# Norm factors spread over the partitions by a transfer and GpSimd instead of TensorE transposes, with the kernel's end regrouped by token blocks

## The chip, the core and the metric

One core of a Trainium2 chip runs the whole program. The metric is the time of one execution on the device in microseconds (us); lower is better. The engines are TensorE (PE in profiles, its weight loads PEld), VectorE (DVE), ScalarE (ACT), GpSimd (POOL) and SyncE (SP, which here only issues transfers).

## What is computed

Two layers of a bidirectional encoder over 512 tokens of 1024 channels, float32, and a last RMSNorm:

```python
def rmsnorm(x, g):
    y = xf * lax.rsqrt(jnp.mean(xf * xf, axis=-1, keepdims=True) + EPS)
    return (y * g).astype(x.dtype)

for l in range(DEPTH):                      # 2
    h = rmsnorm(x, norm1_g[l])
    x = x + gated_parallel_mixer(h, w_in[l], ...)   # three attentions, gates, w_out
    h = rmsnorm(x, norm2_g[l])
    x = x + conv_ffn(h, w_up[l], conv_w[l], conv_b[l], w_down[l])
return rmsnorm(x, final_g)
...
kv = (rmsnorm(c_kv, g_kva) @ w_ukv)         # inside the latent attention (also for c_q)
```

## The kernel before, in words

**Layout.** Activations lie with channels on the 128 partitions and the 512 tokens along the row, so `x` is eight tiles of 128x512. Every weight tile (512 KB at most) comes from HBM on SP's queue into `raw`, is split by ACT into a rounded high part `whi` (L148) and by DVE into the rest `wlo` (L149), and each product is three float32r matmuls per 128 channels, high by high, high by low, low by high (`mm3`, L162 to L164). Three tiles of `raw` and of `whi`/`wlo` are in flight. A matmul of a `wlo` waits for DVE, so whatever stands ahead of an L149 in DVE's queue can hold PE.

**Norms are applied late.** A norm's factor is one number per token. The matmuls run on unscaled input, and DVE multiplies the result by the factors as it leaves PSUM. For that the 512 factors must stand along the row, and the same on all 128 partitions. `rs_tokens` (L185 to L201) adds up the squares over the partitions: four transposes on PE (L191), a reduction on DVE (L193), and small operations on GpSimd (L195 to L200, a power of -0.5 among them). Its result `rt` is 128x4: token 128j+p sits on partition p, column j. `rs_spread` (L203) turns `rt` into the tile `rb` or `rbk`, 128x512: four more transposes on PE of a column repeated 128 times (L208) into one PSUM bank, and a copy by ACT (L209).

**Where `rs_spread` is called.** Three times in a layer, six in all:
- the first norm (`do_lat`, by `norm_spread`): `rb`, first read by DVE in `do_kr` (`ev<-ev,rb`, L155);
- the latent norm (`do_rb_k`): `rbk`, first read in `do_kn(0)` (`ev<-ps_d,rbk`, L155), whose result is split into `kn` (L148, L149) for the scores of `do_ms` (L505 to L509);
- the second norm (`do_up`): `rb`, first read by `conv` (`u<-ps_g,rb`, L155), while PE goes on with further `w_up` tiles.

**Order of the work.** PE's and SP's orders are written out by hand (the list in `schedule`, under `manual_schedule`). The orders on DVE, ACT and GpSimd come from the Tile scheduler, with the weight splits (`fetch`) and the attention steps raised in priority. Each engine works strictly in its order.

**The end.** In the last layer `do_down(1)` hands its last three weight tiles to `finish`. There, for channel tiles m = 1, 2, 3 and halves of 256 tokens, `product` runs 18 matmuls, adds into `x` (DVE L947), squares (ACT L948), adds the squares up (DVE L950) and applies the gain (DVE L951). `total` sums the squares over the partitions by a matmul with a column of ones (L960), `scales` forms mean and power -0.5 on DVE and GpSimd (L965, L967), `turn` transposes 128x128 blocks so that tokens come onto partitions (L955), and `emit` scales two 128x512 halves on ACT and DVE (L971, L972) and sends the rows out (L975 to L978). Token blocks 0 and 1 leave while the last two half products run; blocks 2 and 3 end the program.

Of the kernel before, what the change touches and what calls it, by code (L numbers as in the profile page):

```python
# [10 lines left out]
F32 = mybir.dt.float32  # L11
F32R = mybir.dt.float32r
BF16 = mybir.dt.bfloat16
AF = mybir.ActivationFunctionType
ALU = mybir.AluOpType
AX = mybir.AxisListType

P = 128
L = 2
D = 1024  # L20
S = 512
# [3 lines left out]
EPS = 1e-6  # L25
# [17 lines left out]
def r32(ap):  # L43
    return ap.bitcast(F32)
# [14 lines left out]
class Trunk:  # L59
# [143 lines left out]
    def rs_spread(self, rt, rb):  # L203


        ps = self.bank("r")
        for j in range(4):
            self.nc.tensor.transpose(ps[:, j * P:(j + 1) * P], rt[:, j:j + 1].to_broadcast([P, P]), self.idf)  # L208
        self.nc.scalar.copy(rb, ps)  # L209

    def rope(self, pool, ps, rows, ct, st, nb=2):
        nc = self.nc
# [508 lines left out]
    def do_gq_open(self):  # L721
        nc = self.nc
        self.nps.close()
        self.banks(d=[0, 1], s=[2, 3], tp=[4, 5, 6], po=[7])
        self.gps_, self.gp = self.open("gq")
        gp = self.gp
        rope = gp.tile([P, 2, S], F32, tag="yf", name="rope")
        self.rc, self.rsn = rope[:, 0, :], rope[:, 1, :]
        nc.gpsimd.dma_start(self.rc, self.d["rope"][:, :S])
        nc.gpsimd.dma_start(self.rsn, self.d["rope"][:, S:])  # L730
        self.mul(self.rc, self.rc, self.rb)
        self.mul(self.rsn, self.rsn, self.rb)
        self.sink = self.pr[:, PC_SINK:PC_SINK + 8]
        self.nsink = self.small.tile([P, 8], F32, tag="nsink", name="nsink")
        nc.vector.tensor_scalar(self.nsink, self.sink, -1.0, None, ALU.mult)
        self.gqs = {}

# [154 lines left out]
    def do_down(self, g):  # L892
        nc = self.nc
        if g == 0:
            self.banks(g=[0, 1, 2, 3])
        else:
            self.banks(g=[4, 5, 6, 7])
        ps = [self.bank("g") for _ in range(4)]
        last = self.l == L - 1
        if g == 0 and not last:  # L900
            nc.scalar.activation(self.warm, r32(self.ff[-1][0])[:, 0:1], AF.Exp, scale=0.0)
            self.norm_begin()
        if g == 0 and last:
            self.acc, self.ntags, self.xg = None, ["acc", "sq0", "sq1"], []
        for i, spec in enumerate(self.W["down", g]):
            m, k0, nk = i % 4, spec[1] // P, spec[2]
            if last and (g, k0, m) == (1, 16, 1):
                self.finish([self.weights(sp) for sp in self.W["down", 1][i:]], self.ff[k0:k0 + nk])
                break
            tail = last and g == 1 and m > 0  # L910
            self.mm3(ps[m], self.weights(spec), self.ff[k0:k0 + nk], k0 == 0, k0 == (8 if tail else 16))
            if tail and k0 == 8:
                nc.vector.tensor_add(self.x[4 + m], self.x[4 + m], ps[m])
            if k0 == 16:
                k = 4 * g + m
                nc.vector.tensor_add(self.x[k], self.x[k], ps[m])
                if last:
                    self.acc = self.sumsq(self.const, self.x[k], self.acc, self.ntags)
                    xg = self.const.tile([P, S], F32, tag=f"hh{k}", name="xg")
                    nc.scalar.activation(xg, self.x[k], AF.Copy, scale=self.pr[:, PC_FIN + k:PC_FIN + k + 1])  # L920
                    self.xg.append(xg)
                else:
                    self.norm_piece(k, self.par[self.l + 1][:, PC_G1:PC_G1 + 8])
        if g == 1:
            self.fps.close()

    def finish(self, sts, mv):

        nc = self.nc
        self.banks(z=[1, 2, 3], a=[0, 4, 5, 6], r=[7, 7, 1])
        ps = [None] + [self.bank("z") for _ in range(3)]
        fin = self.pr[:, PC_FIN:PC_FIN + KD]
        for k in range(5, KD):
            self.xg.append(self.const.tile([P, S], F32, tag=f"hh{k}", name="xg"))
        sq = [self.const.tile([P, S], F32, tag=f"hl{k}", name="sq") for k in range(5, KD)]
        outs = [self.fp.tile([P, 2, S], F32, tag="o", name="o", bufs=3) for _ in range(3)]
        outs.append([self.const.tile([P, S], F32, tag=t, name="o") for t in ("hl3", "hl4")])
        rts = self.small.tile([P, 4], F32, tag="rt", name="rts", bufs=3)  # L940
        mss = self.small.tile([P, 4], F32, tag="ms", name="mss", bufs=2)

        def product(m, h):
            k, ts = 4 + m, slice(h * 256, h * 256 + 256)
            self.mm3(ps[m][:, ts], sts[m - 1], [(a[:, ts], b[:, ts]) for a, b in mv])
            x = self.x[k][:, ts]
            nc.vector.tensor_add(x, x, ps[m][:, ts])  # L947
            nc.scalar.activation(sq[m - 1][:, ts], x, AF.Square)  # L948
            if m < 3 or h == 0:
                nc.vector.tensor_add(self.acc[:, ts], self.acc[:, ts], sq[m - 1][:, ts])  # L950
            nc.vector.tensor_scalar(self.xg[k][:, ts], x, fin[:, k:k + 1], None, ALU.mult)  # L951

        def turn(j, hf, ms):
            for m in ms:
                nc.tensor.transpose(tp[j, hf][:, m * P:(m + 1) * P], self.xg[4 * hf + m][:, j * P:(j + 1) * P], self.idf)  # L955

        def total(h, i, src, last=True):
            for j in (0, 1):
                js = slice((2 * h + j) * P, (2 * h + j + 1) * P)
                nc.tensor.matmul(r[h][j][:, 0:1], src[:, js], self.ones[:, 0:1], start=i == 0, stop=last)  # L960

        def scales(h):
            for j in (0, 1):
                c = slice(2 * h + j, 2 * h + j + 1)
                nc.vector.tensor_scalar(mss[:, c], r[h][j][:, 0:1], 1.0 / D, EPS, ALU.mult, ALU.add)  # L965
            hs = slice(2 * h, 2 * h + 2)
            nc.gpsimd.tensor_tensor(rts[:, hs], mss[:, hs], self.neghalf[:, 0:2], ALU.pow)  # L967

        def emit(j):
            o = [outs[j][:, 0, :], outs[j][:, 1, :]] if j < 3 else outs[j]  # L970
            nc.scalar.activation(o[0], tp[j, 0], AF.Copy, scale=rts[:, j:j + 1])  # L971
            nc.vector.tensor_scalar(o[1], tp[j, 1], rts[:, j:j + 1], None, ALU.mult)  # L972
            rows = self.d["out"][j * P:(j + 1) * P, :]
            if j < 3:
                nc.sync.dma_start(rows, outs[j][:].rearrange("p h c -> p (h c)"))  # L975
            else:
                nc.scalar.dma_start(rows[:, :S], o[0])
                nc.sync.dma_start(rows[:, S:], o[1])  # L978

        for m in (1, 2, 3):  # L980
            product(m, 0)
        product(1, 1)
        b = self.bank("r")
        r = [[b[:, 0:S // 2], b[:, S // 2:]]]
        total(0, 0, self.acc)
        scales(0)
        tp = {(j, hf): self.bank("a") for j in (0, 1) for hf in (0, 1)}
        for j, hf in list(tp):
            turn(j, hf, range(4))
        emit(0)  # L990
        emit(1)
        product(2, 1)
        for j, hf in list(tp):
            tp[j + 2, hf] = self.bank("a")
        turn(2, 0, range(4))
        product(3, 1)
        r.append([self.bank("r") for _ in range(2)])
        turn(3, 0, range(4))
        turn(2, 1, range(3))
        total(1, 0, self.acc, False)  # L1000
        total(1, 1, sq[2])
        scales(1)
        turn(3, 1, range(3))
        turn(2, 1, (3,))
        turn(3, 1, (3,))
        emit(2)
        emit(3)


@with_exitstack  # L1010
# [63 lines left out]
```

## Time and profile before

| | before |
|---|---|
| median of 3 runs | 1707.21 us (1707.13 to 1707.24) |
| the profiled execution, its own time | 1707.45 us |
| its span, first to last instruction | 1705.7 us |
| PE busy | 1697.0 us, 99% |
| DVE, ACT, POOL busy | 1147.1, 868.2, 41.8 us (67, 51, 2%) |
| mean granted TensorE clock | 0.999 of full |
| PE waits with a releaser shown | 3 groups: 1.0, 0.8 and 0.3 us in total |

The profile is one execution. Of the 1707.45 us, 1705.7 lie between its first and last instruction, and 1.75 around them. A row of the timeline gives start, duration, engine, line, operation and operands, then in brackets how long the engine stood idle before it and what released it. Matmuls overlap, so their price is read from start to start and not from their durations.

### The profile page before, as it was taken

How to read it: one execution, taken by the hardware profiler on the slowest of the kernel's cores; microseconds unless marked ns; L12 is line 12 of the kernel's file. 1: busy time of each engine (PE TensorE's matmuls, PEld its weight loads, DVE VectorE, ACT ScalarE, POOL GpSimd, SP SyncE). 2: the span in 40 equal slices, each digit the busy share in tenths (PEclk: the TensorE clock that was granted, in tenths of full speed). 3: DMA queues.
4: the chain of work that ended last, by engine and by line, in shares of the span. 5: the costliest groups of instructions: out<-in, count | busy, mean ns of one | idle time of the engine just before them, and what ended most of it. 6: DMA issues, size and time to landing. Idle time of an engine off the chain costs nothing.

```text
span 1705.7 us, 21166 instructions
## 1 busy us (share of the span) xinstructions
PE 1697.0 (99%) x7966; PEld 1420.1 (83%) x7966; DVE 1147.1 (67%) x1873; ACT 868.2 (51%) x1505; POOL 41.8 (2%) x97
## 2 busy tenths in 40 slices
PE   9999999999999999999999999999999999999998
PEld 8888888888888888888888888888888888888887
DVE  6777875887558777734367688768766577777234
ACT  7665655775435444433266556557744444444232
POOL 1110000000000000000010100000000000000000
PEclk9999999999999999999999999999999999999999
DMA  5233233222333333333232232332223333333231
GB/s 177 78 86 82 73 103 87 75 69 74 105 95 103 98 100 99 98 88 101 80 97 79 75 90 69 108 84 69 63 80 111 106 99 99 99 93 94 85 105 68
DMA packets 289206, 155.37 MB, mean 91 GB/s; under 512 B 8816, under 2 KB 285056, under 8 KB 289104
## 3 DMA queue, kind: packets, MB, share of 16 engines
q1 hardware_dynamic: 286752, 148.92, 30.6%
q0 software_dynamic: 2064, 4.82, 0.9%
q8 instruction: 62, 1.02, 0.2%
q14 instruction: 40, 0.33, 0.1%
q10 hardware_dynamic: 288, 0.29, 0.0%
HBM read 151.89 MB, written 2.10 MB: 90 GB/s over the span
## 4 chain that ended last, share of the span: by engine, by line
PE 95%; DVE 1%; issue 1%; ACT 0%; POOLq 0%; POOL 0%; DVEq 0%
PE ps_d L162 21%; PE ps_d L163 21%; PE ps_d L164 21%; PE ps_g L162 7%; PE ps_g L164 7%; PE ps_g L163 7%; PE ps_tp L815 1%; PE ps_po L671 1%; PE ps_tp L656 1%; PE ps_tp L525 1%; PE ps_s L785 1%; PE ps_s L784 1%; PE ps_po L830 1%; PE ps_po L829 1%; PE ps_s L638 0%
## 5 line engine op out<-in xcount | busy, mean ns | idle before, releaser
L148 ACT CAST whi<-raw 128x1024 fp32r<-128x1024 f32 (+4 forms) x339 | 301.4, 889 | 594.3 <-PE ps_d L163 347.0
L162 PE MATMUL ps_d<-hh,whi 128*128 128x512 f32 x1328 | 519.5, 391 | 0.0
L163 PE MATMUL ps_d<-hl,whi 128*128 128x512 f32 x1328 | 517.9, 390 | 0.0
L164 PE MATMUL ps_d<-hh,wlo 128*128 128x512 f32 x1328 | 517.6, 390 | 0.0
L149 DVE TENSOR_TENSOR wlo<-raw,whi 128x1024 fp32r<-128x1024 f32 (+4 forms) x337 | 344.4, 1022 | 183.8 <-ACT whi L148 183.5
L164 PEld LDWEIGHTS ps_d<-hh,wlo 128*128 128x128 f32 x1328 | 249.5, 188 | 52.3
L162 PEld LDWEIGHTS ps_d<-hh,whi 128*128 128x128 f32 x1328 | 249.6, 188 | 50.6 <-DVE rot L155 0.5
L163 PEld LDWEIGHTS ps_d<-hl,whi 128*128 128x128 f32 x1328 | 249.6, 188 | 49.7
L164 PE MATMUL ps_g<-ff,wlo 128*128 128x512 f32 x334 | 130.1, 390 | 0.0
L162 PE MATMUL ps_g<-ff,whi 128*128 128x512 f32 x334 | 130.1, 390 | 0.0
L163 PE MATMUL ps_g<-ff,whi 128*128 128x512 f32 x334 | 130.1, 390 | 0.0
L155 DVE TENSOR_TENSOR u<-ps_d,rb 128x512 f32<-128x512 f32 x80 | 55.3, 691 | 65.1 <-PE ps_d L164 65.1
L155 DVE TENSOR_TENSOR gz<-ps_d,rb 128x512 f32<-128x512 f32 x48 | 33.1, 690 | 84.1 <-PE ps_d L164 84.1
L879 ACT ACTIVATE c<-u,par 128x512 f32<-128x512 f32 x88 | 71.7, 814 | 5.1 <-DVE u L155 2.8
L163 PEld LDWEIGHTS ps_g<-ff,whi 128*128 128x128 f32 x334 | 62.7, 188 | 13.1
L164 PEld LDWEIGHTS ps_g<-ff,wlo 128*128 128x128 f32 x334 | 62.7, 188 | 13.0
L162 PEld LDWEIGHTS ps_g<-ff,whi 128*128 128x128 f32 x334 | 62.7, 188 | 12.8
L149 DVE TENSOR_TENSOR pl<-ps_tp,ph 128x512 fp32r<-128x512 f32 x104 | 68.4, 683 | 3.2 <-ACT ph L148 3.0
L881 DVE SCALAR_TENSOR_TENSOR c<-u,par,c 128x511 f32<-128x511 f32 x88 | 66.0, 750 | 2.7
L885 ACT ACTIVATE c<-c 128x512 f32<-128x512 f32 x44 | 27.8, 631 | 76.6 <-DVE c L881 76.6
L880 DVE SCALAR_TENSOR_TENSOR c<-u,par,c 128x511 f32<-128x511 f32 x88 | 65.5, 745 | 0.6 <-ACT c L879 0.6
L148 ACT CAST ph<-ps_tp 128x512 fp32r<-128x512 f32 x104 | 56.8, 585 | 3.7 <-PE ps_tp L525 2.8
(283 smaller groups left out, 2585.6 us busy)
## 6 DMA issues: line engine op xcount, KB each, us to landing
raw<-in_w_in_dram SPq DMA_DIRECT2D x86, 512.0 KB, 4.0
raw<-in_w_up_dram SPq DMA_DIRECT2D x80, 512.0 KB, 3.9
raw<-in_w_down_dram SPq DMA_DIRECT2D x32, 512.0 KB, 4.3
raw<-in_w_down_dram SPq DMA_DIRECT2D x16, 384.0 KB, 3.6
raw<-in_w_in_dram SPq DMA_DIRECT2D x18, 256.0 KB, 3.0
raw<-in_w_br_mla_dram SPq DMA_DIRECT2D x16, 256.0 KB, 2.8
raw<-in_w_br_na_dram SPq DMA_DIRECT2D x16, 256.0 KB, 2.8
raw<-in_w_br_gqa_dram SPq DMA_DIRECT2D x16, 256.0 KB, 2.8
```

The costliest lines, as they stand in the source:

```text
L148: nc.scalar.copy(hi, src)
L149: nc.vector.tensor_sub(lo, src, r32(hi))
L155: self.nc.vector.tensor_tensor(out, a, b, ALU.mult)
L162: mm(ps, sh, mh, start=first and k == 0, stop=False)
L163: mm(ps, sh, ml, start=False, stop=False)
L164: mm(ps, sl, mh, start=False, stop=last and k == n - 1)
L525: self.nc.tensor.transpose(tp[:, b * P:(b + 1) * P], self.pts[h, b][:, kc * P:(kc + 1) * P], self.idf)
L656: self.nc.tensor.transpose(tp[:, i * P:(i + 1) * P], self.pts["n", h, bp][:, i // 2, (i % 2) * P:(i % 2) * P + P], self.idf)
L879: nc.scalar.activation(c, u, AF.Identity, bias=pr[:, PC_CB + fi:PC_CB + fi + 1], scale=cw[:, 1:2])
L880: nc.vector.scalar_tensor_tensor(c[:, 1:], u[:, :S - 1], cw[:, 0:1], c[:, 1:], ALU.mult, ALU.add)
L881: nc.vector.scalar_tensor_tensor(c[:, :S - 1], u[:, 1:], cw[:, 2:3], c[:, :S - 1], ALU.mult, ALU.add)
L885: nc.scalar.activation(c, c, AF.Gelu_apprx_tanh)
```

## The change

Every call of `rs_spread` now issues a transfer from GpSimd's queue that gathers the 128x4 factors into one row of 512 on partition 0, and one GpSimd instruction that copies that row to all partitions, reading it with a stride of four elements so that the tokens come out in order. The transposes (L208 before) and ACT's copy (L209) are gone. The tile of the row shares the buffer `sq0`. In the program GpSimd also gets an instruction without operands ahead of each broadcast, and another ahead of the next arithmetic on it; these name which library of GpSimd functions (0 or 1) is in use.

The end is regrouped: product 1 runs over all 512 tokens, product 3's second half is added, squared and scaled in blocks of 128 tokens, the factor is a square root on ACT and a reciprocal on DVE for each block (the power on GpSimd goes, and the Sqrt table is loaded at the start of the last `do_down`), four transposes of block 2 move behind the last product, and ACT and DVE follow a written order there. The tile `nsink` moves to another pool.

```diff
     def rs_spread(self, rt, rb):
-        ps = self.bank("r")
-        for j in range(4):
-            self.nc.tensor.transpose(ps[:, j * P:(j + 1) * P], rt[:, j:j + 1].to_broadcast([P, P]), self.idf)
-        self.nc.scalar.copy(rb, ps)
+        row = self.const.tile([P, S], F32, tag="sq0", name="row")
+        self.nc.gpsimd.dma_start(row[0:1, :], rt[:])
+        self.nc.gpsimd.partition_broadcast(rb[:].rearrange("q (j p) -> q j p", p=P),
+                                           row[0:1, :].rearrange("q (p j) -> q j p", p=P))
...
-        self.nsink = self.small.tile([P, 8], F32, tag="nsink", name="nsink")
+        self.nsink = gp.tile([P, 8], F32, tag="nsink", name="nsink")
...
+        if g == 0:
+            nc.scalar.activation(self.warm, r32(self.ff[-1][0])[:, 0:1], AF.Sqrt if last else AF.Exp, scale=0.0)
         if g == 0 and not last:
-            nc.scalar.activation(self.warm, r32(self.ff[-1][0])[:, 0:1], AF.Exp, scale=0.0)
...
-        def scales(h):
-            for j in (0, 1):
-                c = slice(2 * h + j, 2 * h + j + 1)
-                nc.vector.tensor_scalar(mss[:, c], r[h][j][:, 0:1], 1.0 / D, EPS, ALU.mult, ALU.add)
-            hs = slice(2 * h, 2 * h + 2)
-            nc.gpsimd.tensor_tensor(rts[:, hs], mss[:, hs], self.neghalf[:, 0:2], ALU.pow)
+        def scale(c, j, n=1):
+            rt = rts[:, j:j + n]
+            nc.scalar.activation(rt, c, AF.Sqrt, scale=1.0 / D, bias=eps[:, 0:1])
+            nc.vector.reciprocal(rt, rt)
...
-        for m in (1, 2, 3):
-            product(m, 0)
-        product(1, 1)
...
-        product(2, 1)
...
-        turn(2, 0, range(4))
-        product(3, 1)
...
+        product(1, slice(0, S))
...
+        for m in (2, 3):
+            product(m, half[0])
...
+        product(2, half[1])
...
+        product(3, half[1])
+        with self.tc.manual_schedule(engines={mybir.EngineType.Activation, mybir.EngineType.DVE}):
+            for j in (2, 3):
+                add(3, block[j])
+            for j in (2, 3):
+                gain(3, block[j])
+            r = {j: self.bank("r")[:, 0:1] for j in (2, 3)}
+            for j in (2, 3):
+                total(r[j], j, self.acc, True, False)
+            turn(2, 0, range(4))
+            for j in (2, 3):
+                total(r[j], j, sq[2], False, True)
+            turn(2, 1, range(4))
+            for hf in (0, 1):
+                turn(3, hf, range(4))
+            for j in (2, 3):
+                scale(r[j], j)
+            for j in (2, 3):
+                emit(j)
```

**Three places in the order of the work.** First GpSimd around the second norm of layer 0 and the first norm of layer 1. Before, where `ms` is the mean of squares, `rt` the factors and `r` two products of them:

```order
L196 TENSOR_SCALAR ms<-ms 128x4
L198 TENSOR_TENSOR rt<-ms,cst 128x4
L394 DMA rope<-in_rope_dram 128x512
L395 DMA rope<-in_rope_dram 128x512
L196 TENSOR_SCALAR ms<-ms 128x4
```

Now, with `row` the gathered factors and the bare ISA rows those that name a library:

```order
L196 TENSOR_SCALAR ms<-ms 128x4
L198 TENSOR_TENSOR rt<-ms,cst 128x4
L207 DMA row<-rt 1x128x4
L208 ISA
L208 ISA rb<-row 128x512
L394 DMA rope<-in_rope_dram 128x512
L395 DMA rope<-in_rope_dram 128x512
L196 ISA
L196 TENSOR_SCALAR ms<-ms 128x4
```

Between a norm's `rt` and the next work on GpSimd there are now a transfer, two library instructions and the broadcast.

Second, DVE from the reduction of the second norm on, where `wlo` is the low part of a weight tile and `u` the first reader of `rb`. Before:

```order
L193 TENSOR_REDUCE ms<-ps_r 128x4
L149 TENSOR_TENSOR wlo<-raw,whi 128x512 x2
L149 TENSOR_TENSOR wlo<-raw,whi 128x1024
L155 TENSOR_TENSOR u<-ps_g,rb 128x512 x2
L880 SCALAR_TENSOR_TENSOR c<-u,par_75,c 128x511
```

Now:

```order
L193 TENSOR_REDUCE ms<-ps_r 128x4
L149 TENSOR_TENSOR wlo<-raw,whi 128x512 x2
L155 TENSOR_TENSOR u<-ps_g,rb 128x512 x2
L149 TENSOR_TENSOR wlo<-raw,whi 128x1024
L880 SCALAR_TENSOR_TENSOR c<-u,par_75,c 128x511 x2
```

The two readers of `rb` have moved ahead of the first 128x1024 weight split; layer 1 moves the same way.

Third, PE behind the last product, where `cst` is the column of ones, `ps_r` the sums of squares and `ps_a` the transposed blocks. Before, with a `turn` of four ahead of the product:

```order
L955 MATMUL ps_a<-idf,xg 128x128 x7
L960 MATMUL ps_r<-cst,acc 128x1 x2
L960 MATMUL ps_r<-cst,sq 128x1 x2
L955 MATMUL ps_a<-idf,xg 128x128 x5
```

Now:

```order
L968 MATMUL ps_r<-cst,acc 128x1 x2
L965 MATMUL ps_a<-idf,xg 128x128 x4
L968 MATMUL ps_r<-cst,sq 128x1 x2
L965 MATMUL ps_a<-idf,xg 128x128 x12
```

The sums of squares stand nearer to the product's end, and all sixteen transposes of blocks 2 and 3 follow it.

## Rows read from the trace of the kernel before

**Rows 1.** The span with the mean granted TensorE clock, and the page's line of busy time (share of the span, number of instructions).
```profile
core 0: 1705.7 us, clock 0.999
...
PE 1697.0 (99%) x7966; PEld 1420.1 (83%) x7966; DVE 1147.1 (67%) x1873; ACT 868.2 (51%) x1505; POOL 41.8 (2%) x97
```

**Rows 2.** The waits of PE: waiting line, what released it, total us, times, longest us.
```profile
PE ps_r L208 <- POOL rt L200: 0.8, 1, 0.8
```

**Rows 3.** PE's timeline at the second norm of layer 0: the four transposes of the spread and the matmuls behind them.
```profile
506.81 0.60 PE L208 MATMUL ps_r<-idf,rt 128*128 128x128 f32 x4
507.16 0.48 PE L162 MATMUL ps_g<-hh,whi 128*128 128x512 f32 x1
...
507.94 0.39 PE L162 MATMUL ps_g<-hh,whi 128*128 128x512 f32 x1
```

**Rows 4.** The spread of the latent norm in layer 0: the last operation on `rt` on POOL, then PE, the last matmul before the spread, its transposes, the first matmul behind them.
```profile
55.48 0.43 POOL L200 TENSOR_TENSOR rt<-rt 128x4 f32<-128x4 f32 x1
...
54.74 0.39 PE L164 MATMUL ps_d<-whi,yal 128*128 128x512 f32 x1
55.97 0.65 PE L208 MATMUL ps_r<-idf,rt 128*128 128x128 f32 x4 [0.84 <-POOL rt L200]
56.38 0.47 PE L162 MATMUL ps_d<-mg,whi 128*128 128x512 f32 x1
```

**Rows 5.** The second norm of layer 0: POOL's last operation on `rt`; DVE's next weight split and first readers of `rb`; PE's first matmul of the first 128x1024 tile and the first that reads its `wlo`.
```profile
502.94 1.04 POOL L198 TENSOR_TENSOR rt<-ms,cst 128x4 f32<-128x4 f32 x1
...
507.86 1.23 DVE L149 TENSOR_TENSOR wlo<-raw,whi 128x1024 fp32r<-128x1024 f32 x1 [2.45 <-ACT whi L148]
509.01 1.28 DVE L155 TENSOR_TENSOR u<-ps_g,rb 128x512 f32<-128x512 f32 x2
...
512.72 0.39 PE L162 MATMUL ps_d<-hh,whi 128*128 128x512 f32 x1
...
513.17 0.39 PE L164 MATMUL ps_d<-hh,wlo 128*128 128x512 f32 x1
```

**Rows 6.** The latent norm in layer 0, DVE's first reader of `rbk` and the low part of `kn`; PE's first matmul that reads that low part.
```profile
61.18 0.68 DVE L155 TENSOR_TENSOR ev<-ps_d,rbk 128x512 f32<-128x512 f32 x1
...
62.55 0.69 DVE L149 TENSOR_TENSOR kn<-ev,kn 128x512 fp32r<-128x512 f32 x1 [0.36 <-ACT kn L148]
...
66.93 0.39 PE L506 MATMUL ps_s<-kn,qn 128*128 128x512 f32 x1
```

**Rows 7.** The latent norm in layer 1, POOL's last operation on `rt` and the same matmul of PE.
```profile
897.53 0.43 POOL L200 TENSOR_TENSOR rt<-rt 128x4 f32<-128x4 f32 x1
...
910.61 0.39 PE L506 MATMUL ps_s<-kn,qn 128*128 128x512 f32 x1
```

**Rows 8.** The first norm in layer 0: POOL's last operation on `rt`, its next work that needs arithmetic, and DVE's first reader of `rb`.
```profile
23.91 1.03 POOL L198 TENSOR_TENSOR rt<-ms,cst 128x4 f32<-128x4 f32 x1
...
43.73 0.20 POOL L195 TENSOR_TENSOR ms<-ms,r 128x4 f32<-128x4 f32 x1 [15.14 <-DVE ms L193]
...
48.24 0.68 DVE L155 TENSOR_TENSOR ev<-ev,rb 64x512 f32<-64x512 f32 x1
```

**Rows 9.** Prices near those of the new operations. Transfers (queue, count, KB each, median us from issue to landing); a group of POOL's transfer issues (count | busy us, mean ns); POOL's timeline at the program's start, with a library instruction (index 0) between the two rows; the groups of ACT's table loads.
```profile
gmf<-in_gmask_dram POOLq DMA_DIRECT2D x1, 128.0 KB, 2.7
rope<-in_rope_dram SPq DMA_DIRECT2D x2, 256.0 KB, 7.2
...
L562 POOL DMA_DIRECT2D tb<-in_rpb_dram x16 | 9.7, 612 | 157.7 <-PE ps_s L508 120.3 <-DVE tm L622 18.9 <-DVE nm L646 18.4
...
0.72 0.20 POOL masks.py:197 MEMSET idf<- 128x128 f32 x1 [0.29 <-POOLq L1062]
1.00 0.29 POOL masks.py:199 TENSOR_SCALAR_AFFINE_SELECT idf<-idf 128x128 f32<-128x128 f32 x1
...
L885 ACT ACT_TABLE_LOAD x2 | 2.6, 1283 | 3.4 <-DVE c L881 3.4
```

**Rows 10.** PE at the end: the first half product (its first matmul), the sums after four of them, and the first transposes behind the last product.
```profile
1681.41 0.28 PE L162 MATMUL ps_z<-ff,whi 128*128 128x256 f32 x1
...
1690.04 0.50 PE L960 MATMUL ps_r<-cst,acc 128*128 128x1 f32 x4
...
1696.93 0.93 PE L955 MATMUL ps_a<-idf,xg 128*128 128x128 f32 x7
```

**Rows 11.** The chain behind the last product on DVE, ACT, POOL, DVE and SP.
```profile
1697.13 0.42 DVE L947 TENSOR_TENSOR x<-x,ps_z 128x256 f32<-128x256 f32 x1 [1.25 <-PE ps_z L164]
...
1697.58 0.42 ACT L948 ACTIVATE sq<-x 128x256 f32<-128x256 f32 x1 [2.17 <-DVE x L947]
...
1698.47 0.38 DVE L965 TENSOR_SCALAR mss<-ps_r 128x1 f32<-128x1 f32 x2 [0.53 <-PE ps_r L960]
...
1698.93 0.69 POOL L967 TENSOR_TENSOR rts<-mss,cst 128x2 f32<-128x2 f32 x1 [7.31 <-DVE mss L965]
...
1699.66 1.41 DVE L972 TENSOR_SCALAR o<-ps_a,rts 128x512 f32<-128x512 f32 x2 [0.81 <-POOL rts L967]
...
1701.10 0.33 SPq L978 DMA_DIRECT2D out_dram<-o  x1
```

**Rows 12.** Small operations of one column elsewhere in the kernel (count | busy us, mean ns of one).
```profile
L797 ACT ACTIVATE nm<-par,nm 128x1 f32<-128x1 f32 x64 | 18.1, 283 | 0.0
...
L514 DVE RECIPROCAL nm<-nm 128x1 f32<-128x1 f32 x32 | 4.9, 160 | 5.6 <-ACT pt L513 5.2
```

More of the change, by code (lines that the diff above doesn't have):

```diff
@@ L940, in finish, with product, add @@
         rts = self.small.tile([P, 4], F32, tag="rt", name="rts", bufs=3)
-        mss = self.small.tile([P, 4], F32, tag="ms", name="mss", bufs=2)
-        def product(m, h):
-            k, ts = 4 + m, slice(h * 256, h * 256 + 256)
+        eps = self.small.tile([P, 4], F32, tag="ms", name="eps", bufs=2)
+        tp = {}
+        nc.vector.memset(eps, EPS)
+        def product(m, ts):
             self.mm3(ps[m][:, ts], sts[m - 1], [(a[:, ts], b[:, ts]) for a, b in mv])
-            x = self.x[k][:, ts]
+        def add(m, ts):
+            x = self.x[4 + m][:, ts]
@@ L947, in product, with gain, taken @@
             nc.vector.tensor_add(x, x, ps[m][:, ts])
             nc.scalar.activation(sq[m - 1][:, ts], x, AF.Square)
-            if m < 3 or h == 0:
-                nc.vector.tensor_add(self.acc[:, ts], self.acc[:, ts], sq[m - 1][:, ts])
-            nc.vector.tensor_scalar(self.xg[k][:, ts], x, fin[:, k:k + 1], None, ALU.mult)
+        def gain(m, ts):
+            k = 4 + m
+            nc.vector.tensor_scalar(self.xg[k][:, ts], self.x[k][:, ts], fin[:, k:k + 1], None, ALU.mult)
+        def taken(m, ts):
+            nc.vector.tensor_add(self.acc[:, ts], self.acc[:, ts], sq[m - 1][:, ts])
@@ L953, in turn @@
         def turn(j, hf, ms):
+            if (j, hf) not in tp:
+                tp[j, hf] = self.bank("a")
             for m in ms:
-                nc.tensor.transpose(tp[j, hf][:, m * P:(m + 1) * P], self.xg[4 * hf + m][:, j * P:(j + 1) * P], self.idf)
-        def total(h, i, src, last=True):
-            for j in (0, 1):
-                js = slice((2 * h + j) * P, (2 * h + j + 1) * P)
-                nc.tensor.matmul(r[h][j][:, 0:1], src[:, js], self.ones[:, 0:1], start=i == 0, stop=last)
@@ L962, in scales, with total @@
-        def scales(h):
-            for j in (0, 1):
-                c = slice(2 * h + j, 2 * h + j + 1)
-                nc.vector.tensor_scalar(mss[:, c], r[h][j][:, 0:1], 1.0 / D, EPS, ALU.mult, ALU.add)
-            hs = slice(2 * h, 2 * h + 2)
-            nc.gpsimd.tensor_tensor(rts[:, hs], mss[:, hs], self.neghalf[:, 0:2], ALU.pow)
+                nc.tensor.transpose(tp[j, hf][:, m * P:(m + 1) * P], self.xg[4 * hf + m][:, block[j]], self.idf)
+        def total(c, j, src, first, last):
+            nc.tensor.matmul(c, src[:, block[j]], self.ones[:, 0:1], start=first, stop=last)
@@ L978, in emit @@
                 nc.sync.dma_start(rows[:, S:], o[1])
-        for m in (1, 2, 3):
-            product(m, 0)
-        product(1, 1)
[L983 to L989, printed above, removed]
+        half = [slice(0, 256), slice(256, 512)]
+        block = [slice(j * P, (j + 1) * P) for j in range(4)]
+        product(1, slice(0, S))
+        for step in (add, taken, gain):
+            step(1, slice(0, S))
+        for m in (2, 3):
+            product(m, half[0])
+            for step in (add, taken, gain):
+                step(m, half[0])
+        product(2, half[1])
+        for step in (add, taken, gain):
+            step(2, half[1])
+        r = self.bank("r")
+        for j in (0, 1):
+            total(r[:, j:j + 1], j, self.acc, j == 0, j == 1)
+        scale(r[:, 0:2], 0, 2)
+        for j in (0, 1):
+            for hf in (0, 1):
+                turn(j, hf, range(4))
         emit(0)
         emit(1)
-        product(2, 1)
-        for j, hf in list(tp):
-            tp[j + 2, hf] = self.bank("a")
-        turn(2, 0, range(4))
-        product(3, 1)
[L997 to L1007, printed above, removed]
+        product(3, half[1])
[11 more added lines that the diff above has]
+            turn(2, 1, range(4))
+            for hf in (0, 1):
+                turn(3, hf, range(4))
[3 more added lines that the diff above has]
+                emit(j)
 @with_exitstack
```

## The prediction, made before the changed kernel was run

> **What bounds the kernel now.** I read the page's busy times first. PE works 1697.0 of 1705.7 us, at a granted clock of 0.999, and the next engine, DVE, 1147.1 [rows 1]. So the time is PE's list of matmuls, plus what makes PE wait, plus the tail behind its last product. Then PE's waits: behind a spread there is one, 0.8 us, in which it waits for GpSimd's `rt` ahead of L208 in layer 0's latent norm [rows 2]. Last the timelines of the places that the change touches: every instruction taken from PE's list is a gain, and every new wait of PE a loss. The profiled execution took 1707.45 us, 1.75 more than its span and 0.24 more than the median of 1707.21; I sum against it and take 0.24 off at the end.
>
> **Removed: the six spreads on PE.** At a second norm the first of the four transposes starts at 506.81 and the next matmul at 507.16, so they cost 0.35 us. Three matmuls then take 0.78 (507.16 to 507.94) [rows 3], while elsewhere two take 0.45 (512.72 to 513.17) [rows 5], three 0.68: another 0.10 goes with the spread. Six times 0.45 is 2.7 us. In layer 0's latent norm PE also stood: a matmul takes 0.23, so its predecessor from 54.74 was through at 54.97, and the transposes began at 55.97, 1.0 later; they also took 0.41 instead of 0.35 [rows 4]. With that, 3.8 us. ACT's copy goes too, at no gain: ACT is busy 51% [rows 1].
>
> **Added: a transfer and a broadcast on GpSimd.** Let G be the time from `rt` complete to `rb` complete. PE no longer waits for `rt`, but whoever reads `rb` holds DVE's queue, and a weight's low part or `kn` behind it holds PE. How large may G be before PE stands?
> - Second norm, layer 0: `rt` is complete at 503.98 (502.94 + 1.04). By the new order the two `u` (1.28) and then the 128x1024 `wlo` (1.23) run after `rb`, 2.5 us together. PE reads that `wlo` first at 513.17, and 0.45 earlier without the spread, at 512.72 [rows 5]. So `rb` has until 510.2: G may be 6.2. Layer 1 has the same order, and I take 6.2 there too.
> - Latent norm, layer 0: `rt` is complete at 55.91 [rows 4]. From the first reader of `rbk` to the end of `kn`'s low part are 2.06 us (61.18 to 63.24), and PE reads it at 66.93 [rows 6], now 1.5 earlier (1.0 + 0.41 + 0.10). G may be 7.4.
> - Latent norm, layer 1: complete at 897.96, read at 910.61 [rows 7], 0.45 earlier: G may be 10.1.
> - First norm: complete at 24.94, first read at 48.24 [rows 8]: over 20 us. GpSimd's next arithmetic comes at 43.73 [rows 8]; a load, a broadcast and a load back even at 7.2 us a load would end near 45, a microsecond late for a factor that still passes through the rest of that norm. I count nothing.
>
> What is G? The only transfer on GpSimd's queue with a landing listed needed 2.7 us for 128 KB [rows 9]; the new one is 2 KB, in pieces of 16 bytes. Below, the issue alone is 0.6; above, the slowest listed landing is 7.2 [rows 9]. I take 2.7, the same queue. The broadcast writes 512 elements a partition; a 128-wide operation there took 0.29 [rows 9], so I estimate 1.2 (below 0.2, a memset of this width; four-element powers take 1.04 [rows 5]). With 0.1 at each of two hand-overs G is 4.2 if the library instruction costs nothing more.
>
> The disputed cost is that instruction. At the program's start one with index 0 stands between a memset that ends at 0.92 and a select that starts at 1.00 [rows 9], so it cost at most 0.1, but that may be the library already present. The nearest load of code or tables is ACT's table load, 1.28 us [rows 9]. Bounds: 0.1 and, as a fetch from memory, 7.2, the slowest landing. I take 1.3. In GpSimd's list it stands between the transfer's issue and the broadcast, so I expect it to run while the transfer flies: G = 2.05 + load when the load is the longer (issue 0.6, broadcast 1.2, hand-overs), and 4.2 for anything under 2.2. Then no PE stall anywhere: 2.0 us are left at the second norms.
>
> GpSimd's other work behind the broadcast is late by G: the rope transfers of layer 1, whose values are not read before the next layer, and memsets ahead of later attentions. Its 41.8 us of work in the whole span [rows 1] leave room. The load back to library 0 stands ahead of the next norm's first small operation, hundreds of us before the second norms need it. I count nothing for either.
>
> [...]
>
> **The end.** Four half products take 8.63 us (1681.41 to 1690.04), 2.16 each [rows 10]. Product 1 over 512 columns is six times three matmuls at 0.68, 4.08 instead of 4.32: 0.24 saved. Four transposes move from ahead of the last product to behind it, 0.35 by [rows 3]. Together 0.6. Behind the last product, whose end I set at 1696.93, SP issues the last rows at 1701.10 [rows 11], 4.17 later. Between the squares (end 1698.00) and the outputs stand sums, two scalings, and the power on GpSimd, which ends at 1699.62. Now a root on ACT (0.28) and a reciprocal (0.16) [rows 12] with two hand-overs take the place of what lies from 1698.47 to 1699.66: 0.55 instead of 1.19, 0.65 saved. Two adds of 128 columns take about 0.14 more than one of 256, and a square about 0.11 less. Net 0.6. Bounds: 0 (a table load of 1.28 between square and root would take it all) and 1.2 (the whole step gone). The longer run of transposes, 0.35 more, lies beside squares and roots.
>
> The other edits cost nothing: `nsink`'s buffer is written from the same place, and the Sqrt table loads while ACT, 51% busy, has slack.
>
> **Sum.** 3.8 + 0.6 + 0.6 = 5.0 us: 1702.45 against the profile, **1702.2** against the median. About 0.2% (3.4 us) is what a measurement of this kernel can tell from no change.
>
> **Where it tips.** PE's stall is 2(G - 6.2) from the second norms, plus G - 7.4 and G - 10.1 once these are positive. It eats the 5.0 at G = 8.3. Below G = 7.0 the change is faster by over 0.2%, above 9.4 slower by over 0.2%.
>
> **Rivals.**
> - *A, the forecast:* the load is under 4.9 us and beside the transfer, or under 2.8 behind it. 1701.0 to 1703.8; the upper end is G = 7.0, the lower has the end at 1.2 and 0.1 more for each spread. For it: the order of the list, the start of the program. Chance 0.43.
> - *B, the gain is given back:* G between 7.0 and 9.4, as with a load of 5 to 7.2 beside the transfer. At 7.2, G is 9.3 and the stall 2 x 3.1 + 1.9 = 8.1: 1710.3. The new wait is PE on `wlo`, behind `u` in DVE's queue. For it: the load is unseen in the trace and `u` was put ahead of `wlo`. Chance 0.25.
> - *C, slower:* the load starts only at the call, when the row has landed, so G = 4.15 + load. From a load of 5.25 it is slower. At 7.2, G is 11.4 and the stall 2 x 5.2 + 4.0 + 1.3 = 15.7: 1717.9. For it: both instructions come from one call and code may be fetched when first used; against it: the separate instruction ahead of the broadcast. Chance 0.27.
> - *D, the end gives nothing back:* PE's list alone shortens, and the end's 1.2 us go into a table load or the extra transposes: 1703.4. Chance 0.05.
>
> A and D are faster by over 0.2% (0.48), B within (0.25), C slower (0.27). A and D hold no majority over B and C, but their time is the likeliest. A's own range is 1701.0 to 1703.8. The range for 8 in 10 goes up to 1715.0, where G is about 10.9: that leaves out about 0.12 of C above and 0.05 below.
>
> **What would show it.** Right: no L208 on PE, and PE starts the latent scores of layer 0 about 1.5 us earlier; GpSimd's broadcast ends about 4 us behind `rt`; DVE's `u` don't hold PE; the last product ends 4.4 us earlier and SP's last issue follows it by 3.6. B or C: PE waits at L164 for `wlo` near 511 and again in layer 1's second norm, with DVE idle on `u` until GpSimd; the gap between the row's landing and the broadcast's start tells B (none) from C (the load). Wrong altogether: a broadcast of several us without a load, a transfer of 16-byte pieces far over 2.7, or PE waiting at a place not named here. A fall of the granted clock behind a stall, which no row of before shows, would add to B and C.

## The result: slower, by GpSimd's library loads

| | before | changed |
|---|---|---|
| median of 9 runs each | 1707.22 us (1706.65 to 1707.44) | 1712.03 us (1710.64 to 1713.21) |
| the profiled execution, its own time | 1707.45 us | 1711.53 us |
| its span | 1705.7 us | 1709.7 us |

The ratio is 1.0031, with a 95% interval of 1.0023 to 1.0039: slower by about 0.3%, where 1702.2 had been forecast: the other side of no change.

The profile of the changed kernel answers [rows 1] and [rows 2]. First the span and the page's busy times, then PE's waits (what waited, its releaser, total us, times, longest):

```profile
core 0: 1709.7 us, clock 0.999
...
PE 1696.5 (99%) x7924; PEld 1416.8 (83%) x7924; DVE 1145.7 (67%) x1872; ACT 867.1 (51%) x1504; POOL 53.0 (3%) x107
```

```profile
PE ps_d L164 <- DVE wlo L149: 5.7, 2, 2.9
PE idle L338 <- DVE cst L84: 1.0, 1, 1.0
PE ps_s L505 <- DVE pt L512: 0.6, 1, 0.6
```

The wait for `rt` [rows 2] is gone. Two new ones of 2.8 us have come, both for a `wlo`, one at each second norm. The busy line alone would hardly show them: PE's share falls from 99.5% to 99.2%, and the page rounds both to 99%.

Who was late is read on GpSimd's timeline at the second norm of layer 0 (start, duration, engine, line, operation, then the idle time before it and its releaser):

```profile
502.35 1.06 POOL L198 TENSOR_TENSOR rt<-ms,cst 128x4 f32<-128x4 f32 x1
503.71 0.74 POOL L207 DMA_DIRECT2D row<-rt  x1 [0.30 <-POOL rt L198]
511.35 1.21 POOL L208 PARTITION_BROADCAST rb<-row  x1 [6.90 <-issue]
```

`rt` is complete at 503.41 and `rb` at 512.56: G is 9.15 us, not 4.2. The broadcast takes the 1.2 that was estimated. The transfer is no slower than assumed: the page's list has a median of 2.7 us to landing for the six of them, and the chain of releasers has the landing of this one at 506.56 (start, duration, what):

```profile
503.71 2.85 DMA row<-rt
506.56 4.79 issue
511.35 1.22 POOL rb L208
```

What is long is the 6.90 us in which GpSimd waits for nothing that the views show ("issue"): the place of the library instruction. The trace's records, which the views leave out, have it as two MODIFY_POOL_CONFIG of 0.04 us each, at 504.71 and 504.75, well ahead of the landing. Over the six calls the gap is 5.9 to 7.4 us. From `rb` the delay passes on, on DVE and then on PE:

```profile
512.59 1.29 DVE L155 TENSOR_TENSOR u<-ps_g,rb 128x512 f32<-128x512 f32 x2 [7.79 <-POOL rb L208]
...
513.80 1.22 DVE L149 TENSOR_TENSOR wlo<-raw,whi 128x1024 fp32r<-128x1024 f32 x1
```

```profile
511.65 0.39 PE L162 MATMUL ps_d<-hh,whi 128*128 128x512 f32 x1
511.87 0.39 PE L163 MATMUL ps_d<-hl,whi 128*128 128x512 f32 x1
515.07 0.79 PE L164 MATMUL ps_d<-hh,wlo 128*128 128x512 f32 x1 [2.81 <-DVE wlo L149]
515.66 0.63 PE L162 MATMUL ps_d<-hh,whi 128*128 128x512 f32 x1
516.09 0.63 PE L163 MATMUL ps_d<-hl,whi 128*128 128x512 f32 x1
```

In [rows 5] the same `wlo` stood ahead of `u` and was started at 507.86. Here its `whi` was complete at 507.23 (L148 on ACT, 506.18 and 1.05), and it was started at 513.80, behind the two `u`. Behind the pause the matmuls also start 0.43 apart instead of 0.23. The table by stretches says why (busy us and count of PE, PEld, DVE, ACT and POOL, then the granted clock, DMA share, GB/s):

```profile
505.00:512.00 7.00, 7.00 (x33) 5.67 (x31) 0.00 (x0) 1.05 (x1) 0.65 (x1) 1.00 0.32 92
512.00:514.90 2.90, 0.26 (x2) 0.00 (x0) 2.31 (x3) 1.58 (x3) 0.56 (x1) 0.96 0.00 0
514.90:518.20 3.30, 3.13 (x8) 2.51 (x9) 3.30 (x6) 1.82 (x2) 0.00 (x0) 0.52 0.53 156
518.20:525.00 6.80, 6.80 (x32) 5.63 (x31) 6.76 (x11) 4.91 (x6) 0.00 (x0) 1.00 0.55 157
...
1362.20:1366.00 3.80, 3.80 (x17) 3.14 (x18) 3.80 (x6) 1.65 (x3) 0.00 (x0) 1.00 0.46 138
```

After the pause the granted clock is 0.52 until 518.2, which costs another 1.5 us. At the second norm of layer 1 an equal pause leaves it at 1.00. So this part comes and goes.

The same matmuls of the two traces, set side by side, give the whole account (negative: earlier than before): the six spreads -3.7, the end on PE -0.6, behind the last product -0.5; against that the first weights +0.5 (PE's first product starts later), the latent norm of layer 0 +0.9, the second norms +3.0 each, the clock +1.5, small ones +0.3. Together +4.4 in the last issue of SP, 4.3 by the trace.

### The profile page after: what moved, and what is told of

It reads as the page before. It is cut to its first block, busy times and chain, and to the rows that moved or that the text cites. A ratio compares the mean times of both kernels' runs of the same rounds, so it can differ in the third digit from the quotient of the medians.

```text
span 1709.7 us, 21125 instructions
## 1 busy us (share of the span) xinstructions
PE 1696.5 (99%) x7924; PEld 1416.8 (83%) x7924; DVE 1145.7 (67%) x1872; ACT 867.1 (51%) x1504; POOL 53.0 (3%) x107
## 4 chain that ended last, share of the span: by engine, by line
PE 96%; DVE 1%; issue 1%; ACT 0%; POOLq 0%; DMA 0%; POOL 0%; SPq 0%
PE ps_d L164 22%; PE ps_d L162 22%; PE ps_d L163 22%; PE ps_g L164 6%; PE ps_g L163 6%; PE ps_g L162 6%; PE ps_tp L815 1%; PE ps_po L671 1%; PE ps_tp L656 1%; PE ps_g L242 1%; PE ps_tp L525 1%; PE ps_s L785 1%; PE ps_s L784 1%; PE ps_po L830 1%; PE ps_po L829 1%
## 5 line engine op out<-in xcount | busy, mean ns | idle before, releaser
L148 ACT CAST whi<-raw 128x1024 fp32r<-128x1024 f32 (+4 forms) x339 | 301.3, 889 | 580.7 <-PE ps_d L163 337.8
L148 ACT CAST ph<-ps_tp 128x512 fp32r<-128x512 f32 x104 | 56.9, 585 | 3.6 <-PE ps_tp L525 2.8
```

Source lines behind the costliest of these rows:

```text
L148: nc.scalar.copy(hi, src)
```

## Experiments

The theory, L, drawn from the six gaps of 5.9 to 7.4 us: a library instruction costs 6 to 7 us of GpSimd's time when another library is loaded, and runs beside the transfer; G, and with it PE's waits, follow from that alone. Rivals: S, the load is shorter and starts only when the row has landed; T, there is no load, and the transfer and the broadcast are slow by themselves; and that the new end has a part in the loss. Each kernel ran against the kernel before on the same chip, whose median there was 1706.5 to 1706.9.

**The two halves apart.** `spread_only` has the new spread and the old end:

```diff
-        ps = self.bank("r")
...
-        self.nc.scalar.copy(rb, ps)
+        row = self.const.tile([P, S], F32, tag="sq0", name="row")
+        self.nc.gpsimd.dma_start(row[0:1, :], rt[:])
+        self.nc.gpsimd.partition_broadcast(rb..., row...)
```

> The spread by transfer and broadcast with the old end. If the whole loss comes from GpSimd's library loads (theory L: each library instruction ahead of a broadcast takes 6 to 7.4 us and runs beside the transfer, so rb is complete about 9 us after rt and PE stands 3.0 us at each second norm), the time is that of the change plus the 1.1 us that the new end saves: about 1713.1, 1711.8 to 1714.3. If the new end caused the loss, it is below 1704.

Measured: 1713.79 us, ratio 1.0042 (1.0029 to 1.0055). `end_only` is the change with that edit undone:

> The new end with the old spread by transposes. Theory L: 1.1 us below the kernel before (0.6 on PE, 0.5 behind the last product), about 1706.1, and the select at the start of GpSimd begins at 1.0 us as before and not at 9.0. If the end caused the loss: above 1709.

Measured: 1705.24 us, ratio 0.9991 (0.9982 to 1.0000). So the loss sits in the spread, and the rest of the change is a gain, of about 1.5. Not all of that is the end's. PE has no wait for `rt` in the latent norm here, though it still has the transposes, since GpSimd completes that `rt` at 53.30 instead of 55.91 [rows 4]: the 1.0 us of [rows 4] goes without the new spread. The cause shows on DVE in the kernel before:

```profile
31.20 0.17 DVE L735 TENSOR_SCALAR nsink<-par 128x8 f32<-128x8 f32 x1 [3.27 <-DMA par<-in_par_dram]
```

There the operation on `nsink` held DVE's queue for 3.27 us until a transfer of parameters had landed. In `spread_only`, in `end_only` and in the change it stands some 240 us later, and up to the latent norm DVE's order is otherwise the same. The one edit that the two halves share is the move of `nsink` to the other pool; no run moves it alone.

In `spread_only` the clock fell at the other place, the second norm of layer 1 (columns: PE busy, granted clock, DMA share, GB/s):

```profile
1351.00:1357.00 6.00, 6.00 (x29) 1.00 0.31 87
1357.00:1360.10 3.10, 0.37 (x2) 0.89 0.00 0
1360.10:1366.20 6.10, 6.04 (x14) 0.50 0.57 165
1366.20:1372.00 5.80, 5.80 (x27) 0.99 0.33 97
```

There it cost 3 us (14 matmuls in 6.04 us, where 0.23 each make 3.2), and behind the equal pause in layer 0 nothing.

**Load beside the transfer, or behind it?** `second_hop` makes the row land later and leaves GpSimd's order alone:

```diff
+        copy = self.small.tile([P, 4], F32, tag="ms", name="copy", bufs=2)
         row = self.const.tile([P, S], F32, tag="sq0", name="row")
-        self.nc.gpsimd.dma_start(row[0:1, :], rt[:])
+        self.nc.gpsimd.dma_start(copy, rt[:])
+        self.nc.scalar.dma_start(row[0:1, :], copy[:])
```

> The factors are first copied unchanged by a transfer on GpSimd's queue and then gathered by a second one on ACT's queue, so the row lands about 3 us later; GpSimd's order is the same. DVE has the first 128x1024 wlo ahead of u here. Theory L (the load of 6 to 7 us runs beside the transfers): the broadcast at the second norm of layer 0 still starts 7.6 to 8.2 us after rt is complete. Rival S (the load of 4 to 5 us starts when the row has landed): 10.5 to 11.5 us. Rival T (no load, transfers slow by themselves): over 11. By L and S the time is 1704.5 to 1707, since one more product of 5.4 us stands between u and PE's next wait.

Measured: 1705.44 us, ratio 0.9992 (0.9983 to 1.0001). GpSimd's timeline at the second norm of layer 0, and ACT's issue of the second transfer:

```profile
504.12 1.06 POOL L198 TENSOR_TENSOR rt<-ms,cst 128x4 f32<-128x4 f32 x1
505.48 0.74 POOL L208 DMA_DIRECT2D copy<-rt  x1 [0.30 <-POOL rt L198]
513.09 1.21 POOL L210 PARTITION_BROADCAST rb<-row  x1 [6.88 <-issue]
```

```profile
508.28 0.48 ACTq L209 DMA_DIRECT2D row<-copy  x1
```

The gap is 6.88, as it was 6.90, although the row's transfer was issued 3.1 us after `rt` and not 0.3. S and T expected the gap to grow by those 2.8. The broadcast starts 7.9 us after `rt`, as L says. G is 9.1, and yet PE has no wait at the second norms here, because `wlo` stands ahead of `u`. (It waits 2.5 us in the latent norm of layer 0, where ACT's and DVE's order came out otherwise.)

`act_queue` goes the other way, and takes the issue of the transfer out of GpSimd's list:

```diff
-        self.nc.gpsimd.dma_start(row[0:1, :], rt[:])
+        self.nc.scalar.dma_start(row[0:1, :], rt[:])
```

> The change with the gathering transfer issued on ACT's queue, so that GpSimd goes from rt straight to the library instruction. Theory L (the load of 6 to 7 us runs beside the transfer): the broadcast at the second norm of layer 0 starts about 6.9 us after rt is complete instead of 7.95, PE's two stalls shrink by 1.0 each and that in the latent norm goes: 1708.5 to 1710.5. Rival S (the load starts when the row has landed): 7.6 us or more, 1711 to 1713.

Measured: 1705.72 us, ratio 0.9993 (0.9984 to 1.0002). GpSimd's broadcast at the second norm of layer 0, where `rt` is complete at 503.05, and PE's wait:

```profile
508.98 1.21 POOL L208 PARTITION_BROADCAST rb<-row  x1 [5.92 <-issue]
```

```profile
PE ps_d L164 <- DVE wlo L149: 1.5, 2, 0.8
```

The broadcast starts 5.93 us after `rt`, earlier than even L expected: 1.0 for the issue, and the gap itself 1.0 shorter. S is out. The time is 2.8 us below the expected range: G is 7.14, not 8.1, the clock did not fall (mean 1.000 in every execution), and the kernel before is 0.7 us faster on this chip than in the table above.

**No load at all.** `root_factors` computes every factor by a root on ACT and a reciprocal and products on DVE, so that nothing on GpSimd asks for library 0 after the first broadcast:

```diff
-        nc.gpsimd.tensor_scalar(ms, ms, 1.0 / dim, EPS, ALU.mult, ALU.add)
-        nc.gpsimd.tensor_tensor(rt, ms, self.neghalf, ALU.pow)
+        nc.scalar.activation(rt, ms, AF.Sqrt, scale=1.0 / dim, bias=self.eps)
+        nc.vector.reciprocal(rt, rt)
```

> All factors by a root on ACT and a reciprocal and products on DVE, so GpSimd keeps library 1 from the first broadcast on; eight more table loads on ACT. Theory L, and S too: no load at later broadcasts, rb complete 4.0 to 4.6 us after rt, no wait of PE at the second norms, 1702 to 1704.5 (the upper end if table loads hold PE). Rival T: rb still complete about 9 us after rt, PE waits 3 us at each second norm, about 1711.

Measured: 1702.65 us, ratio 0.9975 (0.9965 to 0.9984). GpSimd at the first norm and at the second norm of layer 0, and all of PE's waits:

```profile
37.11 1.24 POOL L210 PARTITION_BROADCAST rb<-row  x1 [7.34 <-issue]
...
502.49 0.54 POOL L209 DMA_DIRECT2D row<-rt  x1 [264.16 <-DVE rt L200]
506.08 1.24 POOL L210 PARTITION_BROADCAST rb<-row  x1 [3.05 <-DMA row<-rt]
```

```profile
PE idle L340 <- DVE cst L84: 1.1, 1, 1.1
PE ps_po L165 <- DVE pl L151: 0.3, 2, 0.2
```

One gap of that size is left, 7.34 us at the first norm, and beside other work. In the second call and later the gap is 1.4 to 3.1 us, in four of the five calls put down to the row's landing, and here `rb` is complete 4.8 us after the issue began. From `rt` it is 5.1 us, half a microsecond over what was expected, as the transfer took longer to land than in the change (median 3.3 us). T is out: the transfer and the broadcast need no more than that. This kernel is faster than the kernel before and than the change.

**The order on DVE.** `split_first` leaves the loads as they are, records the readers of `rb` later, and has DVE follow the written order in that group:

```diff
-            self.group(..., {(0, 3): self.norm_sums, (1, 1): lambda: (self.norm_spread(), conv(0, 1)),
-                             (1, 2): lambda: conv(2), (1, 3): lambda: conv(3)})
+            with self.tc.manual_schedule(engines={mybir.EngineType.DVE}):
+                self.group(..., {(0, 3): self.norm_sums, (1, 1): self.norm_spread,
+                                 (1, 3): lambda: conv(0, 1)})
+            conv(2, 3)
```

> The change with one edit: the readers of rb are recorded behind the last product of the second norm's group, and DVE follows the written order in that group, so the first two 128x1024 wlo stand ahead of u in DVE's queue. Theory L: GpSimd does the same (rb complete about 9.1 us after rt), but PE no longer waits for wlo at the second norms (6.0 us less) and the clock has no pause to fall after (0 to 2.5 less): 1704 to 1706.5, with a wait of at most 1 us left in the latent norm. If the late rb itself cost the time, whatever the order: no change, 1712.

Measured: 1703.72 us, ratio 0.9981 (0.9973 to 0.9990). DVE at the second norm of layer 0:

```profile
506.75 1.23 DVE L149 TENSOR_TENSOR wlo<-raw,whi 128x1024 fp32r<-128x1024 f32 x1 [2.46 <-ACT whi L148]
509.47 1.23 DVE L149 TENSOR_TENSOR wlo<-raw,whi 128x1024 fp32r<-128x1024 f32 x1 [1.49 <-ACT whi L148]
512.08 0.69 DVE L155 TENSOR_TENSOR u<-ps_g,rb 128x512 f32<-128x512 f32 x1 [1.38 <-POOL rb L208]
```

`rb` is as late as in the change (complete 9.16 us after `rt`), and it costs PE nothing. The time is 0.3 us below the expected range; the kernel before is 0.7 us faster on this chip, as for `act_queue`. Late data alone was no loss; what stood behind the waiting instruction on its queue was.

**The clock.** `filled_wait` gives PE work for the length of the pause, in both layers:

```diff
+            if self.fill:
+                ps = self.bank("r")
+                for _ in range(12):
+                    self.nc.tensor.matmul(ps, self.h[0][0][:, 0:P], self.h[0][0], start=True, stop=True)
+                self.fill = False
             self.conv(fi, self.dense(self.spec(), self.h))
```

> The change with twelve matmuls of 128x512 whose result nobody reads, ahead of the first product behind the second norm's group, in both layers: PE works 2.7 us where it stood 2.8. The stall by wlo is the same in length. Theory L with a clock that falls after the pause in some runs (1.2 to 3 us each time): granted clock 1.00 behind both places, all runs within 1 us of each other, 1710.3 to 1711.2. If the runs' spread of 2.5 us has another cause (the loads, the transfers): the spread and the median of 1712.0 stay.

Measured: 1709.92 us (1708.96 to 1710.63 over 11 runs), ratio 1.0018 (1.0010 to 1.0027). The stretches at both places:

```profile
512.00:514.80 2.80, 2.80 (x14) 2.33 (x13) 1.97 (x3) 1.24 (x2) 0.80 (x1) 1.00 0.00 0
514.80:520.00 5.20, 5.13 (x23) 3.90 (x23) 5.20 (x8) 3.06 (x4) 0.00 (x0) 1.00 0.44 126
...
1360.30:1366.00 5.70, 5.60 (x25) 4.31 (x24) 5.70 (x9) 3.55 (x5) 0.00 (x0) 1.00 0.45 134
```

Twenty-four matmuls that nobody needs (5.4 us) stand in the pauses, the clock stays at 1.00, and the kernel is 3.4 us above the kernel before of its chip, where the change was 4.8 above. The median is 0.4 us below the expected range, on the same chip. The spread is 1.7 us against 2.6; under 1 was expected, so a part of it has another source. The change's own runs say the same of the clock: the three from 1710.6 to 1710.9 have a mean of 0.999, the five from 1712.0 to 1713.2 one of 0.996 to 0.998.

**The start.** In the profile of the change GpSimd's select, which begins at 1.00 before [rows 9], begins at 9.03:

```profile
9.03 0.28 POOL masks.py:199 TENSOR_SCALAR_AFFINE_SELECT idf<-idf 128x128 f32<-128x128 f32 x1 [8.10 <-issue]
```

In `spread_only`, whose last GpSimd work is the old end's power (library 0), it begins at 1.23; in the change, `filled_wait` and `act_queue`, whose last GpSimd work is a broadcast, at 9.03, 9.90 and 9.88. `split_reset` and `root_reset` add one product on GpSimd at the end of `split_first` and `root_factors`:

```diff
+        nc.gpsimd.tensor_tensor(self.neghalf, self.x[4][:, 0:4], self.x[4][:, 0:4], ALU.mult)
```

> split_first with one product of 128x4 on GpSimd behind the last broadcast, so that each execution ends with library 0 loaded as those of the kernel before do. Theory L, with a library that stays loaded from one execution to the next: the select at GpSimd's start begins near 1.0 us instead of 9 to 10, and the weights that PE waits for at 5 us come up to 0.5 us earlier: 1702.8 to 1703.8 beside split_first's 1703.7. If the wait of 8 to 9 us at the start comes from the second library being in the program at all: the select stays at 9 to 10 us.

> root_factors with the same product on GpSimd at the end. The select at GpSimd's start begins near 1.0 us, and the time is that of root_factors, 1702.65, or up to 0.5 us less: 1701.9 to 1702.9. If the second library in the program alone makes the start slow: the select at 9 to 10 us.

Measured: 1703.26 us, ratio 0.9979 (0.9970 to 0.9989), and 1702.20 us, ratio 0.9975 (0.9965 to 0.9984). The select in both:

```profile
1.22 0.29 POOL masks.py:199 TENSOR_SCALAR_AFFINE_SELECT idf<-idf 128x128 f32<-128x128 f32 x1 [0.29 <-POOL idf masks.py:197]
```

So the start goes with what GpSimd ran last in a kernel: behind a broadcast GpSimd stood idle ahead of the select for 8.1 to 9.0 us, behind a product for 0.29. L reads this as a library that stays loaded from one execution to the next, and the 8 us as the load back to library 0. That the second library in the program makes the start slow by itself is out: both reset kernels have it. In time the pairs differ by some 0.5 us (1703.72 to 1703.26, on two chips, and 1702.65 to 1702.20), inside the runs' spread, and that the load at the start costs it is not shown: PE's wait for the first weights, 0.4 us in the change, stands in `end_only` and `root_reset` too, whose select is early, and not in `root_factors`, whose select is late.

## Why the prediction failed

**The step that failed is the price of the library instruction.** I took 1.3 us, from ACT's table load, between bounds of 0.1 and 7.2; the gaps under "issue" were 5.9 to 7.4, at the upper bound, and 6.9 at the second norms. The row that I leaned on for the low end, the start of the program [rows 9], showed an instruction for a library that, as the select at 1.22 in the two reset kernels has it, the execution before had left in place; I had named that possibility and still let it weigh.

**The forecast's rival B is what happened, not C.** The load runs beside the transfer, which `second_hop` (gap 6.88, with the row issued 2.8 us later) and `act_queue` (broadcast 5.93 us after `rt`) show. B put G at 9.3 and the time at 1710.3, under a load of 7.2; G was 9.15, and the change's lowest run is 1710.64. I gave it 0.25 and called it "within", because its sum came out under 0.2%. What it lacked was the clock: behind one of the two pauses the granted clock fell to 0.52 in the change's profile, which cost 1.5 us, and to 0.50 in that of `spread_only`, which cost 3; with the pauses filled the loss is 3.4 us instead of 4.8. I had named that as an addition to B and C, without a price, since no row of before had a pause like it. The top of the stated range, 1715.0, belongs by the prediction's own sum to G = 10.7, not 10.9; nothing hangs on it.

**At the second norms the slack was right to a tenth.** PE's stall was to be G - 6.2 at a second norm. The change: G 9.15 and 9.19, so 2.95 and 2.99; PE fell back by 2.97 and 3.02. `act_queue`: G 7.14 and 7.04, so 0.94 and 0.84; measured 0.95 and 0.87. In the latent norm of layer 0 the size came out (limit 7.4, G 8.19, so 0.8; lost 0.9), by luck, for the place did not: `rt` was complete 1.4 earlier than before, so `kn` was in time, and PE waited 4 us later, at L505, for DVE's `pt`, behind a queue on DVE that had waited 2.87 us for `rbk`. I had put the move of `nsink` at nothing; it goes with that earlier `rt`. In layer 1 the limit of 10.1 was not reached (8.5), and no wait stands there. The load back to library 0, behind the first norm's broadcast, came about when it was expected (two MODIFY_POOL_CONFIG in the trace's records, at 38.43 and 38.46, then 7.01 us idle), and none of PE's waits names it: DVE had that `ms` ready at 42.15, and GpSimd, done with the broadcast at 38.50, took it at 45.52 (the row names DVE's `acc`, which this operation does not read):

```profile
41.47 0.68 DVE L193 TENSOR_REDUCE ms<-ps_r 128x4 f32<-128x512 f32 x1
```

```profile
37.26 1.24 POOL L208 PARTITION_BROADCAST rb<-row  x1 [7.35 <-issue]
45.52 0.65 POOL L195 TENSOR_TENSOR ms<-ms,r 128x4 f32<-128x4 f32 x1 [7.01 <-DVE acc L181]
```

**The gains were right too.** Per spread PE gained 0.43 to 0.45, and 1.5 in the latent norm of layer 0, as the sum had it, though `end_only` shows that 1.0 of it comes without the new spread. On PE the end gave 0.6. Behind the last product the changed kernel looks like this on PE, ACT, DVE and SP, to be set beside [rows 11]:

```profile
1701.71 0.50 PE L968 MATMUL ps_r<-cst,acc 128*128 128x1 f32 x4
```

```profile
1703.02 0.48 ACT L972 ACTIVATE rts<-ps_r,eps 128x1 f32<-128x1 f32 x2 [0.27 <-PE ps_r L968]
```

```profile
1703.31 0.39 DVE L973 RECIPROCAL rts<-rts 128x1 f32<-128x1 f32 x2 [0.52 <-ACT rts L972]
1703.74 1.62 DVE L978 TENSOR_SCALAR o<-ps_a,rts 128x512 f32<-128x512 f32 x2
```

```profile
1705.39 0.33 SPq L984 DMA_DIRECT2D out_dram<-o  x1
```

SP's last issue follows the last product by 3.68 us instead of 4.17 (forecast 3.6): no table load came between square and root (the trace's last is at 1586.42), two adds of 128 columns took 0.286 each against 0.421 for one of 256, and the squares 0.302 against 0.416. With the load out of the way, `root_reset` is 4.7 us below the kernel before on its chip; the sum had said 5.0.

## What to carry to other kernels

When a step moves to an engine that loads code, look first at what that engine ran just before and will run just after: here the step, the broadcast, took 1.2 us, and the gaps at the switch 5.9 to 7.4 there and 7.0 back. If the switch can't be avoided, ask what stands behind the waiting reader in its queue; moving two weight splits ahead of it was worth 7 to 8 us here, with the data as late as ever. And a pause on TensorE may cost more than its length, as here 1.5 us more behind one of 2.8 and nothing more behind the other, so a forecast with such a pause in it wants a term for the clock.

## What the runs showed of the hardware

- A switch of GpSimd's library showed as idle time under "issue": 5.9 to 7.4 us at the six broadcasts of the change, and at the program's start 8.10 us there, 8.97 in `filled_wait` and 8.96 in `act_queue`. The 7.01 us behind the first norm's broadcast, taken as the load back, are put down to another releaser. It went on beside a transfer in flight: a row issued 2.8 us later left the gap at 6.88, and without the issue ahead of it the broadcast started 2.0 us earlier. Directly behind the issue of a transfer the gap at the second norms was 6.9, without one 5.9; why is open.
- No such gap where GpSimd had used the same library last: 1.4 to 3.1 us at the second and later calls of `root_factors`, and at the start the select at 1.22 us in the two reset kernels instead of 9.03 in the change.
- The broadcast of a row of 512 float32 to 128 partitions took 1.21 to 1.27 us in the change, read with a stride of four elements; the gathering transfer of 2 KB, 16 bytes from each partition, had a median of 2.7 us to landing on GpSimd's queue there (2.5 to 4.5), 3.3 in `root_factors`, and 3.1 on ACT's in `act_queue`.
- After equal pauses of 2.8 us TensorE's granted clock stayed at 1.00 (layer 1 of the change) or was 0.52 over 3.3 us (layer 0 of the change) or 0.50 over 6.1 us (layer 1 of `spread_only`). What decides it is open.
